# Wider start-up streams, x's splits ahead of the weights' and an earlier bias table in a two-layer decoder step

## The chip, the cores and the metric

The kernel runs on one core of a Trainium2 chip. The metric is the device time of one execution in microseconds (us), the median of several runs; it is compared with the median of the kernel before. All shares and moments below are of one profiled execution and count from its first instruction.

## What is computed

The reference is one inference step of a decoder trunk of two layers on 256 prompt tokens and 8 sample tokens (264 columns in all), model width 1024, in float32. Each layer projects x by one wide matrix, runs three mixers, gates and merges them, and ends with a SwiGLU block:

```python
u = x @ w_in
(q_r, k_r, v_r, g_r, z, xbc, dt_raw, q_c, k_c, v_c, gates) = jnp.split(u, _offsets(IN_SIZES), axis=-1)
# retention on q_r, k_r, v_r; SSD on xbc, dt; sliding-window attention on q_c, k_c, v_c:
bias = rel_bias[_t5_bucket(jnp.maximum(dist, 0))].astype(F32)
logits = jnp.where(mask[None, :, None, None], s + bias, -1e30)
...
mix = (g_a * br_a + g_b * br_b + g_c * br_c) @ w_out
x = _layer_norm(ALPHA * x + mix, ln1_g, ln1_b)
ffn = (jax.nn.silu(x @ w_ffn_gate) * (x @ w_ffn_up)) @ w_ffn_down
x = _layer_norm(ALPHA * x + ffn, ln2_g, ln2_b)
```

The bias of the sliding window is a table over distance, one row of 383 values for each of 8 heads, shared by both layers.

## The kernel before

Everything is held transposed: 128 channels on the partitions, the 264 tokens as columns. To keep float32 accuracy every product is made of three matmuls in a reduced format (`mm3`): a high part times a high part, high times low, low times high. So each weight block and each block of x is first split into a high part, written by ScalarE (`wh`, `xh`), and a remainder, written by VectorE (`wl`, `xl`). A unit of a projection is 128 output channels: 8 blocks of x times 3 matmuls of 264 columns, 24 matmuls, gathered in one PSUM bank.

Weights come by strips of 1 MB (or two halves of 0.5 MB) through SyncE's queue into 4 strip buffers (`strip`); the queue's next strip is issued when a buffer is released by its splits. Small loads, the states and all stores go through GpSimd's queue, in the order of the program.

The start of the program, `load_x`, loads an identity (`cst`), the two halves of the prompt (`xt`) and the sample rows (`xts`). While they travel, TensorE runs 32 matmuls of a constant 128 by 128 tile with itself (`ps_warm`); their result is never read. Then x is transposed block by block (`ps_x`: two transposes of 128 columns and a narrow one for each of 8 blocks; four PSUM banks), and each block is split. The first projections are `w_kv` (2 units) and `w_qc` (4 units), by `halves`: each strip holds four of the eight blocks of x. Behind them come `params` (`ps_par`, `ps_head`), `w_v` (4 units) and `w_qk` (8 units).

`bias_table` is a generator in three pieces: it loads its small inputs; then multiplies the relative bias by a one-hot matrix (`ps_rb`), copies the row to `brow`, makes the sample tokens' bias (`ps_bs`, `bias_s`), stores the row to DRAM (`bias_row`) and spreads it there over 128 rows for each head (`bias`, two transfers of four heads each). `swa`, the window attention, reads `bias` back in a skewed pattern (`bias_t`, two transfers) and adds it to the scores `ps_sc`.

A scheduler that goes by its own timing model sets the order of the instructions on each engine at build time; `high_priority` and `issue_after` in the code are its hints. On the chip each engine then keeps that order. `pump` advances the queue of side work (`bias_table`, `swa` and others) between units.

Of the kernel before, what the change touches and what calls it, by code (L numbers as in the profile page):

```python
# [30 lines left out]
NEG = -1e30  # L31
RSCALE = 128**-0.5

WARM = 32
CONV = 1536

QR, KR, VR, GR, ZZ, XBC, DT, QC, KC, GATE = 0, 512, 1024, 1536, 2048, 3072, 4608, 4624, 5136, 5392
# [69 lines left out]
class Kern:  # L107
# [118 lines left out]
        self.mm(ps, wl, xh, False, last)  # L226

    def xsplit(self, h, l, src):
        self.act(h, src)
        self.sub(l, src, h.bitcast(F32))  # L230

    def gemm(self, w, x, ps, first=True, last=True):

# [6 lines left out]
    def load_x(self):  # L240
        nc, a, cp = self.nc, self.a, self.cp
        keep = _OFF["onehot"][0]
        self.cst = cp.tile([128, keep], F32, name="cst")
        nc.sync.dma_start(self.cst[:, 0:256], a["cst"][:, 0:256])

        self.xb = [self.xp.tile([128, KB, T + 2], F32R, name=f"x{c}") for c in "hl"]
        self.xw = [tuple(t[:, k] for t in self.xb) for k in range(KB)]
        self.x = [(h[:, :T], lo[:, :T]) for h, lo in self.xw]
        xt = [self.T4("xt")[:, :D] for _ in range(2)]
        xs = self.T4("xts")[:NS, :D]  # L250
        nc.sync.dma_start(xt[0], a["x_prompt"][0, 0:128])
        nc.sync.dma_start(xt[1], a["x_prompt"][0, 128:256])
        nc.sync.dma_start(xs, a["x_sample"][:, 0])
        self.neg = cp.tile([128, 128], F32R, name="neg")
        nc.vector.memset(self.neg.bitcast(F32), -1.0 / 128)
        self.par = [None] * DEPTH
        ps = self.pg("ps_warm")
        for _ in range(WARM):
            self.mm(ps[:, :128], self.neg, self.neg)
        bias = self.bias_table()  # L260
        next(bias)
        self.queue.append(bias)
        for k in range(KB):
            ps = self.pm("ps_x")
            for c in range(2):
                self.tr(ps[:, c * 128 : (c + 1) * 128], xt[c][:, k * 128 : (k + 1) * 128])
            self.tr(ps[:, SEQ:T], xs[:, k * 128 : (k + 1) * 128])
            with self.tc.high_priority(400):
                self.xsplit(*self.x[k], ps[:, :T])
        self.pump(1)  # L270
        self.eps = cp.tile([128, 2], F32, name="eps")
        self.alpha = [cp.tile([128, 128], F32R, name=f"al{c}") for c in "hl"]
        h, lo = self.alpha
        self.act(h, self.c("ident"), scale=ALPHA)
        self.stt(lo, self.c("ident"), ALPHA, h.bitcast(F32), ALU.mult, ALU.subtract)
        nc.vector.memset(self.eps[:, 0:1], EPS)
        nc.vector.memset(self.eps[:, 1:2], 4.0 * EPS)
# [37 lines left out]
    def bias_table(self):  # L315

        nc, a = self.nc, self.a
        keep = _OFF["onehot"][0]
        cs0 = self.T2("cs0")[:, : _CST.shape[1] - keep]
        self.ld(cs0, a["cst"][:, keep:])  # L320
        oh, sel = cs0[:32, 0:129], cs0[:8, 129:257]
        rb = self.S([32, 8], "rb")
        self.ld(rb, a["rel_bias"])
        row = self.T2("brow")[:8, :385]
        nc.gpsimd.memset(row[:, :383], NEG)
        self.ld(row[:, 383:385], a["sinks"].rearrange("l h -> h l"))
        yield
        ps = self.pm("ps_rb")
        self.mm(ps[:8, :129], rb, oh)
        nc.vector.tensor_copy(out=row[:, 127:256], in_=ps[:8, :129])  # L330

        self.bias_s = self.cp.tile([128, 131], F32, name="bias_s")
        ps = self.pm("ps_bs")
        self.mm(ps[:, :129], sel, row[:, 127:256])
        self.mm(ps[:, 129:131], sel, row[:, 383:385])
        self.act(self.bias_s, ps[:, :131])

        once = self.dp.tile([8, 383], F32, name="bias_row")
        self.ld(once, row[:, :383])
        self.bias = self.dp.tile([8, 128, 383], F32, name="bias")  # L340
        for h in range(0, 8, 4):
            self.ld(self.bias[h : h + 4], once[h : h + 4].unsqueeze(1).to_broadcast([4, 128, 383]))
        yield


# [210 lines left out]
    def mixers(self, l):  # L556
# [10 lines left out]
        def halves(c0, n, name, pieces, shape):  # L567

            pss = [self.pg("ps_u") for _ in range(n)]
            for i in range(2):  # L570
                raw = self.strip([(0, 128, self.win(l, c0, n * 128)[:, 4 * i : 4 * i + 4])], (4, n * 128), name)
                for u in range(0, n, 2):
                    ws = self.wsplits([pieces(raw, u + v) for v in range(2)], shape)
                    if n == 2:

                        for k in range(4):
                            for v in range(2):
                                x = self.x[4 * i + k]
                                self.mm3(pss[v][:, :T], *(w[:, k] for w in ws[v]), *x, i + k == 0, i == 1 and k == 3)
                        continue  # L580
                    for v in range(2):
                        self.gemm(ws[v], self.x[4 * i : 4 * i + 4], pss[u + v][:, :T], i == 0, i == 1)
# [520 lines left out]
    def swa(self, l):  # L1103
# [28 lines left out]
        for half in range(2):  # L1132
            lgs.append(self.T8("lg")[:, :1536])
            bias = self.T4("bias_t")[:, :1024].rearrange("p (h j) -> p h j", h=4)
            o = self.bias.offset + half * 4 * 128 * 383 + 127
            self.ld(bias, bass.AP(tensor=self.bias.tensor, offset=o, ap=[[382, 128], [128 * 383, 4], [1, 256]]))
            biases.append(bias)
        for t in range(4):

# [538 lines left out]
```

## Time and profile before

| | us |
|---|---|
| median of 3 runs | 1091.47 (1088.8 to 1091.77) |
| the profiled execution | 1088.66 |
| its span, first to last instruction | 1086.9 |
| TensorE busy | 1068.3 (98%) |
| VectorE busy | 840.1 (77%) |
| ScalarE busy | 662.4 (61%) |
| GpSimd busy | 163.4 (15%) |
| TensorE's granted clock, mean share of full speed | 0.997 |

A matmul's busy time includes the way through the array and overlaps the next one's, so the distance between two starts, not the duration, tells the pace. A time in brackets behind a row is the idle time of the engine before it, with what ended it.

### The profile page before, as it was taken

To read this page: it belongs to the slowest core of one execution; us is meant where nothing else is said; L and a number is where in the kernel's file an instruction comes from. 1 tells how busy PE (TensorE), PEld (TensorE's weight loads), DVE (VectorE), ACT (ScalarE), POOL (GpSimd) and SP (SyncE) were. 2 spreads that over 40 slices of the span, in tenths; PEclk is the share of its full clock that TensorE was granted. 3 is DMA by queue.
4 is the path that set the end of the run, shared out by engine and by line. 5 is a ranking of instruction groups with operands and counts; after the bars stand their busy time and mean duration, and the time that the engine had idled before them with its cause. 6 is when DMAs were issued, how large, how long until landed. Compare 5 with 4: busy or idle time off the path is not lost.

```text
span 1086.9 us, 22192 instructions
## 1 busy us (share of the span) xinstructions
PE 1068.3 (98%) x8619; PEld 1029.9 (95%) x8619; DVE 840.1 (77%) x1904; ACT 662.4 (61%) x1332; POOL 163.4 (15%) x248
## 2 busy tenths in 40 slices
PE   9999999999999999999999999999999999999998
PEld 7988998999999999999999899889999999999996
DVE  3588885898868997777599888478886899877654
ACT  3476556667646776665467855366675558666452
POOL 3300012522001011221020001153100000222300
PEclk9999999999999999999999999999999999999999
DMA  9854555994455678899675344669855546989951
GB/s 313 258 175 153 158 145 180 246 273 164 155 194 156 219 247 287 290 312 317 198 254 171 127 156 128 194 160 301 247 183 174 176 149 207 291 286 298 324 183 41
DMA packets 176826, 230.74 MB, mean 212 GB/s; under 512 B 8040, under 2 KB 151984, under 8 KB 176544
## 3 DMA queue, kind: packets, MB, share of 16 engines
q1 hardware_dynamic: 156384, 166.95, 47.6%
q0 software_dynamic: 20272, 62.34, 19.6%
q8 instruction: 68, 1.11, 0.4%
q14 instruction: 38, 0.31, 0.1%
q10 hardware_dynamic: 64, 0.03, 0.0%
HBM read 213.52 MB, written 19.61 MB: 214 GB/s over the span
## 4 chain that ended last, share of the span: by engine, by line
PE 61%; issue 26%; DMA 6%; DVE 3%; POOL 2%; ACT 1%; POOLq 0%; DVEq 0%; ACTq 0%
PE ps_gate L125 12%; PE ps_fg L125 10%; PE ps_fu L125 10%; PE ps_br L125 7%; PE ps_fd L125 6%; PE ps_z L125 5%; PE ps_o L125 4%; PE ps_u L125 4%; DMA bias<-bias_row 2%; DMA rs<-in_state_ret_dram 1%; PE ps_y L125 1%; DVE wl L146 1%; DMA vb<-scr_v 1%; PE ps_var L125 1%; DMA out_dram<-sn 1%
## 5 line engine op out<-in xcount | busy, mean ns | idle before, releaser
L125 PE MATMUL ps_u<-xh,wh 128*128 128x264 f32 x608 | 176.1, 291 | 3.1 <-ACT wh L141 1.8
L125 PE MATMUL ps_u<-xl,wh 128*128 128x264 f32 x608 | 176.4, 290 | 0.0
L125 PE MATMUL ps_u<-xh,wl 128*128 128x264 f32 x608 | 175.6, 291 | 0.1
L125 PEld LDWEIGHTS ps_u<-xh,wh 128*128 128x128 f32 x608 | 116.1, 192 | 6.5 <-ACT wh L141 2.3
L125 PEld LDWEIGHTS ps_u<-xh,wl 128*128 128x128 f32 x608 | 116.5, 192 | 2.1 <-issue 1.7
L125 PEld LDWEIGHTS ps_u<-xl,wh 128*128 128x128 f32 x608 | 116.3, 191 | 1.1 <-issue 0.5
L125 PE MATMUL ps_gate<-xh,wh 128*128 128x264 f32 x384 | 110.1, 290 | 2.2 <-ACT th L141 2.2
L125 PE MATMUL ps_gate<-xl,wh 128*128 128x264 f32 x384 | 109.4, 288 | 0.0
L125 PE MATMUL ps_gate<-xh,wl 128*128 128x264 f32 x384 | 108.9, 288 | 0.0
L125 PE MATMUL ps_fd<-fh,wl 128*128 128x264 f32 x352 | 100.4, 285 | 0.0
L125 PE MATMUL ps_fd<-fh,wh 128*128 128x264 f32 x352 | 100.3, 285 | 0.0
L125 PE MATMUL ps_fd<-fl,wh 128*128 128x264 f32 x352 | 100.0, 284 | 0.0
L125 PE MATMUL ps_fg<-xl,wh 128*128 128x264 f32 x288 | 82.5, 286 | 1.0 <-DVE xl L158 1.0
L169 POOL DMA_DIRECT2D s<-in_state_ssm_dram x32 | 28.8, 900 | 362.4 <-ACT sn L141 229.1
L141 ACT ACTIVATE wh<-w_gate 128x1024 fp32r<-128x1024 f32 x48 | 50.6, 1057 | 53.5 <-PE ps_br L125 19.8
L146 DVE TENSOR_TENSOR wl<-w_fd,wh 128x1024 fp32r<-128x1024 f32 (+1 forms) x48 | 54.2, 1136 | 36.6 <-ACT wh L141 36.5
L125 PE MATMUL ps_fu<-xh,wh 128*128 128x264 f32 x288 | 82.4, 286 | 0.0
L125 PE MATMUL ps_fg<-xh,wh 128*128 128x264 f32 x288 | 82.0, 285 | 0.3 <-DVE v L158 0.3
L125 PE MATMUL ps_fu<-xl,wh 128*128 128x264 f32 x288 | 82.1, 285 | 0.0
L125 PE MATMUL ps_fu<-xh,wl 128*128 128x264 f32 x288 | 81.8, 284 | 0.0
L125 PE MATMUL ps_fg<-xh,wl 128*128 128x264 f32 x288 | 81.7, 284 | 0.0
L141 ACT ACTIVATE wh<-w_fd 128x1024 fp32r<-128x1024 f32 (+1 forms) x48 | 47.1, 986 | 54.8 <-PE ps_fd L125 46.2
(458 smaller groups left out, 3416.0 us busy)
## 6 DMA issues: line engine op xcount, KB each, us to landing
w_gate<-in_w_in_dram SPq DMA_DIRECT2D x24, 1024.0 KB, 5.4
w_fg<-in_w_ffn_gate_dram SPq DMA_DIRECT2D x22, 1024.0 KB, 5.2
w_fu<-in_w_ffn_up_dram SPq DMA_DIRECT2D x22, 1024.0 KB, 6.3
s<-in_state_ssm_dram POOLq DMA_DIRECT2D x32, 512.0 KB, 7.0
w_fd<-in_w_ffn_down_dram SPq DMA_DIRECT2D x16, 1024.0 KB, 8.9
out_dram<-sn POOLq DMA_DIRECT2D x24, 512.0 KB, 7.7
w_qk<-in_w_in_dram SPq DMA_DIRECT2D x8, 1024.0 KB, 9.4
w_xs<-in_w_in_dram SPq DMA_DIRECT2D x8, 1024.0 KB, 5.0
```

The source lines that it names most:

```text
L125: return self.nc.tensor.matmul(out, lhsT, rhs, start=start, stop=stop).ins
L141: i = self.nc.scalar.activation(out=out, in_=in_, func=func, scale=scale, **kw)
L146: return self.nc.vector.tensor_tensor(out=out, in0=a, in1=b, op=op).ins
L169: return self.nc.gpsimd.dma_start(out, in_).ins
```

## The change

Four edits stand together.

- The 32 matmuls of 128 columns become 16 of 512 columns: the moving operand is the same tile four times, by a broadcast access.
- `xsplit` returns its two instructions; those of block 1 of x are kept as `self.after`, and the first split of `halves` is made to stand behind them in the order.
- The generator's second piece is pumped ahead of the last block's transposes, not after all of them, and a third piece is cut off: what makes `bias_s` now comes behind the stores to DRAM.
- `bias` becomes two DRAM tiles of four heads each, so that a load of `bias_t` depends on one of the two stores.

```diff
-WARM = 32
+WARM = 16
...
     def xsplit(self, h, l, src):
-        self.act(h, src)
-        self.sub(l, src, h.bitcast(F32))
+        return self.act(h, src), self.tt(l, src, h.bitcast(F32), ALU.subtract)
...
         for _ in range(WARM):
-            self.mm(ps[:, :128], self.neg, self.neg)
+            self.mm(ps.rearrange("p (a b) -> p a b", a=4), self.neg, self.neg.unsqueeze(1).to_broadcast([128, 4, 128]))
...
         for k in range(KB):
+            if k == KB - 1:
+                self.pump(1)
...
-                self.xsplit(*self.x[k], ps[:, :T])
-        self.pump(1)
+                i = self.xsplit(*self.x[k], ps[:, :T])
+            if k == 1:
+                first = i
+        self.after = first
...
-        self.bias = self.dp.tile([8, 128, 383], F32, name="bias")
-        for h in range(0, 8, 4):
-            self.ld(self.bias[h : h + 4], once[h : h + 4].unsqueeze(1).to_broadcast([4, 128, 383]))
+        self.bias = [self.dp.tile([4, 128, 383], F32, name=f"bias{h}") for h in range(2)]
+        for h in range(2):
+            self.ld(self.bias[h], once[4 * h : 4 * h + 4].unsqueeze(1).to_broadcast([4, 128, 383]))
+        yield
...
-                    ws = self.wsplits([pieces(raw, u + v) for v in range(2)], shape)
+                    with ExitStack() as es:
+                        for j in self.after:
+                            es.enter_context(self.tc.issue_after(j))
+                        ws = self.wsplits([pieces(raw, u + v) for v in range(2)], shape)
+                    self.after = ()
```

The lines on `once` and `bias` now stand ahead of those that make `bias_s`, with the new `yield` between.

TensorE at the start of the program, before (`ps_warm` the constant streams, `ps_x` the transposes of x, `ps_u` the first projections):

```order
L125 MATMUL ps_warm<-neg 128x128 x32
L129 MATMUL ps_x<-cst,xt 128x128 x7
L129 MATMUL ps_x<-cst,xts 128x8 x3
L129 MATMUL ps_x<-cst,xt 128x128
L129 MATMUL ps_x<-cst,xts 128x8
L125 MATMUL ps_u<-xh,wh 128x264 x2
L129 MATMUL ps_x<-cst,xt 128x128 x2
L129 MATMUL ps_x<-cst,xts 128x8
L125 MATMUL ps_u<-xl,wh 128x264
```

The same place now:

```order
L125 MATMUL ps_warm<-neg 128x512 x16
L129 MATMUL ps_x<-cst,xt 128x128 x8
L129 MATMUL ps_x<-cst,xts 128x8 x4
L129 MATMUL ps_x<-cst,xt 128x128 x2
L129 MATMUL ps_x<-cst,xts 128x8
...
L125 MATMUL ps_u<-xh,wh 128x264
L125 MATMUL ps_u<-xl,wh 128x264
L125 MATMUL ps_rb<-cs_111,rb 8x129
```

Seven blocks of x are transposed ahead of the first projection, where four were; the bias row's matmul `ps_rb` is third behind them, where 21 matmuls of `ps_u` stood ahead of it.

ScalarE at the same place, before (`wh` and `xh` are high parts):

```order
L141 ACTIVATE alh<-cst 128x128
L141 ACTIVATE wh<-w_kv 128x512 x4
L141 ACTIVATE xh<-ps_x 128x264 x4
L141 ACTIVATE wh<-w_qc 128x512 x2
L141 ACTIVATE xh<-ps_x 128x264 x4
```

and now:

```order
L141 ACTIVATE alh<-cst 128x128
L141 ACTIVATE xh<-ps_x 128x264 x4
L141 ACTIVATE wh<-w_kv 128x512 x2
L141 ACTIVATE xh<-ps_x 128x264
L141 ACTIVATE wh<-w_kv 128x512 x2
L141 ACTIVATE xh<-ps_x 128x264 x2
L141 ACTIVATE wh<-w_qc 128x512 x4
L141 ACTIVATE xh<-ps_x 128x264
```

The first four blocks of x moved ahead of all weights; VectorE's remainders follow the same order.

GpSimd's queue behind the first loads, before (`bias_t` is the read of the table; `ctok` and `kvs` are the new cache rows on their way out):

```order
L169 DMA bias_row<-brow 8x383
L169 DMA bias<-bias_row 512x1x383 x2
L169 DMA bias_t<-bias 128x4x256 x2
L169 DMA kcache<-in_cache_swa_k_dram 128x8x128
```

and now:

```order
L169 DMA bias_row<-brow 8x383
L169 DMA bias_165<-bias_row 512x1x383
L169 DMA bias_166<-bias_row 512x1x383
L165 DMA out_dram<-ctok 128x128 x2
L165 DMA out_dram<-kvs 8x128 x2
L169 DMA bias_t<-bias_165 128x4x256
L169 DMA bias_t<-bias_166 128x4x256
L169 DMA kcache<-in_cache_swa_k_dram 128x8x128
```

Four stores moved ahead of the reads of the table. SyncE's queue has the same transfers in the same order.

## Rows read from the trace of the kernel before

**Rows 1.** The page, part 1: busy us (share of the span) xinstructions.

```profile
PE 1068.3 (98%) x8619; PEld 1029.9 (95%) x8619; DVE 840.1 (77%) x1904; ACT 662.4 (61%) x1332; POOL 163.4 (15%) x248
```

**Rows 2.** Chain that ended last, by time: start, us, what.

```profile
399.73 2.93 PE ps_fu L125 x24
```

**Rows 3.** Timeline of TensorE, start of the program: start, us, engine, line, operation.

```profile
1.06 7.09 PE L125 MATMUL ps_warm<-neg 128*128 128x128 f32 x32 [1.06 <-DVE neg L255]
7.94 1.72 PE L129 MATMUL ps_x<-cst,xt 128*128 128x128 f32 x7
...
11.95 0.81 PE L125 MATMUL ps_u<-xh,wh 128*128 128x264 f32 x2 [1.27 <-ACT xh L141]
...
24.89 0.42 PE L125 MATMUL ps_u<-xh,wh 128*128 128x264 f32 x1
25.11 0.42 PE L125 MATMUL ps_u<-xl,wh 128*128 128x264 f32 x1
...
25.52 0.29 PE L125 MATMUL ps_u<-xh,wh 128*128 128x264 f32 x1
...
39.14 0.25 PE L129 MATMUL ps_par<-cst,par_rows 100*128 100x100 f32 x1
```

**Rows 4.** Windows: engines' busy us (xinstructions), granted clock, DMA share, GB/s.

```profile
20.00:22.00 2.00, 2.00 (x9) 1.34 (x9) 0.71 (x2) 0.00 (x1) 0.00 (x0) 1.00 1.10 350
687.60:691.00 3.40, 1.33 (x23) 0.93 (x27) 0.81 (x1) 1.44 (x2) 0.87 (x1) 1.00 0.67 200
691.00:694.40 3.40, 3.40 (x28) 3.02 (x25) 0.43 (x1) 0.28 (x1) 0.91 (x2) 0.51 1.12 344
76.70:80.10 3.40, 2.52 (x22) 2.27 (x21) 2.28 (x6) 3.36 (x11) 0.00 (x0) 1.00 0.00 0
```

**Rows 5.** One window, of `ps_u`'s instructions alone (no POOL column).

```profile
11.95:25.50 13.55, 10.54 (x39) 9.00 (x40) 0.00 (x0) 0.00 (x0) 1.00 1.04 331
```

**Rows 6.** Timeline of TensorE, layer 2, as a wait ends at 691 us.

```profile
692.14 0.42 PE L125 MATMUL ps_br<-chl,wl 128*128 128x264 f32 x1
692.36 0.64 PE L125 MATMUL ps_br<-chl,wh 128*128 128x264 f32 x2
```

**Rows 7.** Timeline of TensorE, transposes of the attention weights (`ps_pT`).

```profile
77.03 1.48 PE L129 MATMUL ps_pT<-cst,lg 128*128 128x128 f32 x12
```

**Rows 8.** Timeline of ScalarE, splits at the start.

```profile
9.05 1.15 ACT L141 ACTIVATE wh<-w_kv 128x512 fp32r<-128x512 f32 x2 [5.78 <-DMA w_kv<-in_w_in_dram]
...
11.53 1.22 ACT L141 ACTIVATE xh<-ps_x 128x264 fp32r<-128x264 f32 x4
...
33.32 1.06 ACT L141 ACTIVATE wh<-w_v 128x1024 fp32r<-128x1024 f32 x1 [1.79 <-PE ps_u L125]
```

**Rows 9.** Timeline of VectorE, remainders at the start.

```profile
9.71 2.71 DVE L146 TENSOR_TENSOR wl<-w_kv,wh 128x512 fp32r<-128x512 f32 x4 [6.12 <-ACT wh L141]
12.34 1.45 DVE L146 TENSOR_TENSOR xl<-ps_x,xh 128x264 fp32r<-128x264 f32 x4
```

**Rows 10.** Timeline of GpSimd: issues of the bias table's transfers.

```profile
22.17 0.51 POOL L169 DMA_DIRECT2D bias_row<-brow  x1 [9.54 <-DVE brow L330]
27.53 2.24 POOL L169 DMA_DIRECT2D bias<-bias_row  x2 [4.85 <-DMA bias_row<-brow]
42.65 0.81 POOL L169 DMA_DIRECT2D bias_t<-bias  x1 [12.87 <-issue]
```

**Rows 11.** DMA issues, 0 to 75 us: count, KB each, median us to landing.

```profile
w_v<-in_w_in_dram SPq DMA_DIRECT2D x2, 1024.0 KB, 14.6
bias<-bias_row POOLq DMA_DIRECT2D x2, 766.0 KB, 15.2
xt<-in_x_prompt_dram SPq DMA_DIRECT2D x2, 512.0 KB, 5.5
bias_t<-bias POOLq DMA_DIRECT2D x2, 512.0 KB, 6.3
```

**Rows 12.** DMA by queue, 33 to 44 us: packets, MB, share of 16 engines.

```profile
q1 hardware_dynamic: 1545, 1.56, 51.6%
```

More of the change, by code (lines that the diff above doesn't have):

```diff
@@ L330, in bias_table @@
         nc.vector.tensor_copy(out=row[:, 127:256], in_=ps[:8, :129])
+        once = self.dp.tile([8, 383], F32, name="bias_row")
+        self.ld(once, row[:, :383])
+        self.bias = [self.dp.tile([4, 128, 383], F32, name=f"bias{h}") for h in range(2)]
+        for h in range(2):
+            self.ld(self.bias[h], once[4 * h : 4 * h + 4].unsqueeze(1).to_broadcast([4, 128, 383]))
+        yield
         self.bias_s = self.cp.tile([128, 131], F32, name="bias_s")
@@ L336, in bias_table @@
         self.act(self.bias_s, ps[:, :131])
-        once = self.dp.tile([8, 383], F32, name="bias_row")
-        self.ld(once, row[:, :383])
-        self.bias = self.dp.tile([8, 128, 383], F32, name="bias")
-        for h in range(0, 8, 4):
-            self.ld(self.bias[h : h + 4], once[h : h + 4].unsqueeze(1).to_broadcast([4, 128, 383]))
         yield
@@ L1134, in swa @@
             bias = self.T4("bias_t")[:, :1024].rearrange("p (h j) -> p h j", h=4)
-            o = self.bias.offset + half * 4 * 128 * 383 + 127
-            self.ld(bias, bass.AP(tensor=self.bias.tensor, offset=o, ap=[[382, 128], [128 * 383, 4], [1, 256]]))
+            b = self.bias[half]
+            self.ld(bias, bass.AP(tensor=b.tensor, offset=b.offset + 127, ap=[[382, 128], [128 * 383, 4], [1, 256]]))
             biases.append(bias)
```

## The prediction

> **What bounds the kernel now.** I read the page first: TensorE is busy for 1068.3 of 1086.9 us [rows 1], so a change pays where it shortens TensorE's own row of work or one of its waits. Then the timeline of TensorE from the start of the program, for the distance between starts. In the middle of the program 24 matmuls of 264 columns take 2.93 us, 0.122 us each [rows 2]. In the first 25 us the same matmul starts every 0.22 us, and only at 25.5 us does its duration drop from 0.42 to 0.29 us [rows 3]. The same 0.22 us stands in layer 2 at 692 us [rows 6], in a stretch whose granted clock is given as 0.51 [rows 4]: that is the 1.2 GHz level, and 0.122 us belongs to the 2.4 GHz level. (The clock column reads 1.00 at the start too [rows 4, 5]; the spacing contradicts it, and I go by the spacing.) So all of the start, up to 25.5 us, runs at the low level, the 32 constant streams and the first projections alike. From 11.95 to 25.5 us TensorE gets through 39 matmuls of `ps_u` [rows 5] that would cost 39 × 0.122 = 4.8 us at the high level.
>
> What the engine did before the clock rose: 7.1 us of streams of 128 columns did not raise it; transposes mixed with `ps_u` did not; `ps_u` back to back did, up to 25.5 us. Before 691 us TensorE was busy for only 1.33 of 3.4 us [rows 4], and then it fell.
>
> The last views were ScalarE's and VectorE's timelines, for the splits that the first `ps_u` waits for [rows 8, 9], and the transfers behind them [rows 10 to 12].
>
> **The streams.** 32 streams of 128 columns take 7.09 us, 0.22 us each [rows 3]. A stream of 512 columns at the low level is an estimate from the 264-column spacing: 512 / 264 × 0.22 = 0.43 us, so 16 of them take 6.8 us: from 1.06 to 7.9 us, as now, or less if the clock rises among them. Nothing is lost there. The second half of x, 5.5 us after its issue [rows 11], arrives at about 7.2 us in any case. What changes is that the engine streams columns without pause, as the `ps_u` did that raised the clock. I expect it to rise before 7.9 us.
>
> **The start of the projections.** Now the first `ps_u` starts at 11.95 us, after 1.27 us of waiting for an `xh` [rows 3]; that `xh` stood behind four `wh` of `w_kv`, which ran from 9.05 us, when the weights had landed [rows 8]. After the change: 12 transposes from 7.2 to 7.9 us on, 1.48 us at the high level by the 12 transposes of `ps_pT` [rows 7], 2.7 us at the low one (seven take 1.72 us [rows 3]); then four `xh`, 1.22 us [rows 8], of which the first starts once its own block is transposed; then one `wh` of 0.62 us. That is 8.4 + 1.2 + 0.6 = 10.2 us at best, 10.9 us at worst; I take 10.5 us. The transposes of blocks 4 to 6, now ahead of `ps_u`, wait for PSUM banks that `xl` releases (four take 1.45 us [rows 9]) and end in the same time, so they hide behind the splits.
>
> **From there to the end of `w_qc`.** In both orders exactly 144 matmuls of `ps_u` (48 of `w_kv`, 96 of `w_qc`) stand ahead of `ps_par`, which now starts at 39.14 us [rows 3]. At the high level they take 144 × 0.122 = 17.6 us. Add 0.3 us for `ps_rb`, 0.35 us for the last block's transposes, 0.7 us of waiting for the first `wl` (0.69 us of VectorE, four in 2.71 us [rows 9]) and 0.3 us for later splits: 10.5 + 17.6 + 1.65 = 29.75 us, or **9.4 us earlier**. `ps_bs` moves behind `ps_par` and takes back 0.3 us. The splits keep up: per half strip of `w_qc` ScalarE needs 4 × 0.53 us and VectorE 4 × 0.6 us, against 48 × 0.122 = 5.9 us of matmuls.
>
> **What is late next: `w_v`.** Both strips of `w_v` are there at 27 us (the second is issued at 12.4 us and takes 14.6 us [rows 11]), while its first split runs at 33.32 us, held by TensorE and not by the transfer [rows 8]. After the change that split is wanted at 28 to 29 us. And here the other edit meets it. The bias table's stores, issued at 27.53 us and 15.2 us in flight [rows 10, 11], move up with `ps_rb` to about 18 us, on top of the strips. While they run, SyncE's queue moves 1.56 MB in 11 us [rows 12], 0.14 MB/us, where everything together moves 350 GB/s without them [rows 4]. With 2.8 MB still to come for `w_v` at 19 us (8 us to 27 us at 0.35), the first strip would land between 24 us (no hindrance) and 31 us (0.14 throughout): a wait of 0 to 2 us. I take 1.0 us. It cannot be below nothing.
>
> **The table's own path.** The reads `bias_t` now stand behind four stores of `ctok` and `kvs` on GpSimd. These wait for the first values of `w_v`, so the reads go out at about 38 us instead of 42.65 and land 6.3 us later [rows 10, 11], at 44 to 46 us. The third pair of score matmuls `ps_sc` needs the banks that the first pair's addition frees, and stands 74 matmuls of `ps_u` behind: at about 47 us. The margin is 0 to 3 us; I take a wait of 0.5 us.
>
> **The rest.** Behind about 175 us the two orders agree but for neighbours that changed places; between 45 and 175 us the scheduler wrote the side work in a different order. The same work, the same lengths: 0, with ±1.5 us, the size of the waits of that stretch.
>
> **The sum**: −9.4 + 0.3 + 1.0 + 0.5 = −7.6 us. Against the profiled execution, 1088.66 us, that is 1081.1 us; the median, 1091.47 us, lies 2.8 us above that execution, so I put the median after at 1083.9 us.
>
> **Rivals.** *The clock falls again in the transposes.* Between the streams and the first `ps_u` lie some 3 us in which TensorE only transposes. For it: nothing but transposes would hold the clock there. Against it: from 76.7 to 80.1 us TensorE did 22 matmuls of which 12 are transposes in one row, was busy for 2.52 of 3.40 us, and the granted clock stayed at 1.00 [rows 4, 7]. If it falls, a low stretch follows as at 691 us, 3.4 us [rows 4], or twice that, and gives away half of it: 1.7 to 3.4 us, for 1086 to 1087 us. This is what the Trainium skill says in "TensorE: Matmul & The Clock Gate", Part 4: transposes do not count as busy for the clock. By that rule the sum would be −5 us instead of −7.6; the window at 76.7 us speaks against it, though not purely, since ordinary matmuls lie in it too.
>
> *The streams do not raise the clock*, so the change does not do what it says. Then the transposes take 2.7 us, ScalarE starts `wh` later than now, the first `ps_u` runs at about 12 us at the low level, and the clock rises only behind a dense stretch of `ps_u`, as it did before; with the transposes out of the way I put that at about 17 us instead of 25.5 us: 23 matmuls at 0.22 us, 121 at 0.122 us, 1.5 us of the small things. `ps_par` comes at 33.3 us, 5.8 us earlier; less 1.8 us as above, 1087.5 us.
>
> *The strips are the bound.* If the table's stores hold the queue down for 15 us and `w_v` and `w_qk` all come late, each of the two can cost 2 to 3 us: −9.4 + 0.3 + 5 + 0.5 = −3.6, 1088 us.
>
> *Slower: the table comes late.* If the two stores, fighting with 3.8 MB of strips, take 30 us instead of 15.2, `bias_t` lands near 60 us. VectorE stands at the addition with the `wl` of `w_qk` queued behind it, and TensorE at `ps_sc`. The wait starts to count when the read lands after 47 us and eats the whole gain after 54 us; at 60 us it would be 13 us, less 9 us of gain, 1095 us.
>
> **How the numbers follow.** A measurement of this kernel tells about 0.3%, 3.3 us, from no change: faster means under 1088.2 us. Forecast 0.57 (1083.9, its ends 1080 and 1087); clock falls 0.20 (1086.5); streams idle 0.07 (1087.5); strips bound 0.10 (1088); late table 0.06 (1095). The first four lie mostly under 1088.2: 0.56 + 0.17 + 0.04 + 0.05 = 0.82 faster; the rest of them, 0.12, within; 0.06 slower. The range 1080 to 1088.5 leaves out the late table, a part of the strips, and what is better than the lower ends of the costs.
>
> **What would show it.** The spacing of the `ps_warm` streams falling from 0.43 to 0.22 us among them; `ps_u` starting at 10.5 us with starts 0.122 us apart; `ps_par` near 30 us; no wait of the first `ps_u` of `w_v` over 2 us. Wrong would be a first `ps_u` spacing of 0.22 us (the clock), a wait on `w_v`'s strip (the stores), or a `ps_par` near 30 us with an unchanged span (the gain given back later).

## The result, and the profile after

The median after the change is 1085.88 us (1082.21 to 1092.02) beside 1093.17 us (1088.8 to 1099.89) for the kernel before in the same runs: a ratio of 0.9943, with an interval of 0.9924 to 0.9963. The ratio is taken over all runs of both kernels and not from the two medians, whose quotient is 0.9933. The medians lie 7.3 us apart; the forecast was 1083.9 us in a range of 1080 to 1088.5. The profiled execution took 1083.71 us (span 1081.9 us), 5.0 us less than that of before.

The page, part 1, against [rows 1]: TensorE is busy for 5.3 us less, with the 16 streams fewer, and still for 98% of the span.

```profile
PE 1063.0 (98%) x8603; PEld 1023.0 (95%) x8603; DVE 838.8 (78%) x1904; ACT 661.4 (61%) x1332; POOL 163.8 (15%) x248
```

TensorE's timeline of the kernel after, the same places as [rows 3] (start, us, engine, line, operation, and in brackets the wait ahead of it):

```profile
1.06 6.24 PE L125 MATMUL ps_warm<-neg 128*128 128x512 f32 x16 [1.06 <-DVE neg L254]
7.13 1.03 PE L129 MATMUL ps_x<-cst,xt 128*128 128x128 f32 x8
...
9.27 0.44 PE L129 MATMUL ps_x<-cst,xt 128*128 128x128 f32 x2 [0.76 <-DVE xl L146]
...
10.84 0.39 PE L125 MATMUL ps_u<-xh,wh 128*128 128x264 f32 x1
...
11.82 0.28 PE L125 MATMUL ps_u<-xl,wh 128*128 128x264 f32 x1
11.94 0.28 PE L125 MATMUL ps_u<-xh,wl 128*128 128x264 f32 x1
...
30.29 0.25 PE L129 MATMUL ps_par<-cst,par_rows 100*128 100x100 f32 x1
```

Two `ps_u` behind each other start 0.12 us apart from 11.82 us on (11.82 and 11.94), where before they stood 0.22 us apart up to 25.5 us. The trace's own record of the granted clock rises at 6.0 us, among the streams; in before it rises at 25.47 us. `ps_par`, behind the same 144 `ps_u`, comes at 30.29 instead of 39.14 us: 8.85 us earlier.

ScalarE and GpSimd of the kernel after, against [rows 8] and [rows 10]:

```profile
8.36 1.24 ACT L141 ACTIVATE xh<-ps_x 128x264 fp32r<-128x264 f32 x4 [5.05 <-PE ps_x L129]
...
27.06 1.06 ACT L141 ACTIVATE wh<-w_v 128x1024 fp32r<-128x1024 f32 x1 [3.27 <-PE ps_u L125]
...
13.03 0.51 POOL L169 DMA_DIRECT2D bias_row<-brow  x1
21.28 2.25 POOL L169 DMA_DIRECT2D bias<-bias_row  x2 [7.75 <-DMA bias_row<-brow]
...
39.85 1.56 POOL L169 DMA_DIRECT2D bias_t<-bias  x2
```

The four `xh` now run at 8.36 us, ahead of every `wh`. The first split of `w_v` waits for TensorE's `ps_u`, not for a transfer. The table's stores go out at 21.28 instead of 27.53 us, its reads at 39.85 us.

The 8.85 us do not all last. I took the start of TensorE's n-th matmul behind the streams in each trace (both have 8587 of them) and subtracted: at the 1350th (171.56 us after, 180.17 us before) the kernel after is 8.62 us ahead, at the 1400th (182.58 and 187.94 us) only 5.36 us, at the 4000th 5.24, at the 8500th 4.53 us. So 3.3 us are lost between 171 and 183 us. There TensorE's timeline of the kernel after reads:

```profile
171.56 1.09 PE L129 MATMUL ps_rt<-cst,on 128*128 128x128 f32 x4
173.16 1.48 PE L129 MATMUL ps_rt<-cst,on 128*128 128x128 f32 x4 [0.52 <-DVE gg L146]
174.47 0.27 PE L129 MATMUL ps_craw<-cst,craw 128*36 128x128 f32 x1
...
176.01 0.39 PE L125 MATMUL ps_gate<-xh,wh 128*128 128x264 f32 x1 [1.15 <-ACT th L141]
...
177.00 0.42 PE L125 MATMUL ps_gate<-xh,wh 128*128 128x264 f32 x1
```

And its windows (busy us of each engine, then granted clock, DMA share, GB/s):

```profile
173.20:176.70 3.50, 2.18 (x11) 1.35 (x12) 2.60 (x5) 3.47 (x8) 0.00 (x0) 1.00 0.18 54
176.70:180.10 3.40, 3.40 (x18) 3.32 (x17) 2.54 (x3) 2.04 (x5) 1.93 (x4) 0.50 0.69 262
```

The same place in before:

```profile
180.15 0.27 PE L129 MATMUL ps_rt<-cst,on 128*128 128x128 f32 x1
...
180.38 0.93 PE L129 MATMUL ps_rt<-cst,on 128*128 128x128 f32 x7
...
182.91 0.39 PE L125 MATMUL ps_gate<-xh,wh 128*128 128x264 f32 x1 [1.12 <-ACT th L141]
```

From the first of retention's eight transposes `ps_rt` to the `ps_craw` behind them 2.9 us pass after the change (171.56 to 174.47 us) and 1.2 us before (180.15 to 181.39 us, with one `ps_gate` among them). The `ps_gate` behind them waits for ScalarE's `th` in both kernels, 1.15 and 1.12 us, so this wait is no part of the loss. Then, after the change alone, 3.4 us run at the low level: a `ps_gate` takes 0.42 us again, as `ps_u` did at the start of before.

The order of TensorE's row says why the transposes wait: between the last `ps_qkv` of the retention's norm and the first `ps_rt` stand 19 `ps_gate` after the change and 38 before. ScalarE writes the eight inputs `on` of the transposes, with a split of `w_gate` between the fifth and the sixth (kernel after):

```profile
170.40 1.86 ACT L141 ACTIVATE on<-ps_ro,nb,rrr 128x128 f32<-128x128 f32 x5 [0.77 <-DVE nb L158]
172.13 1.07 ACT L141 ACTIVATE wh<-w_gate 128x1024 fp32r<-128x1024 f32 x1
173.08 1.18 ACT L141 ACTIVATE on<-ps_ro,nb,rrr 128x128 f32<-128x128 f32 x3
```

The last `on` ends at 174.26 us, 5 us behind that `ps_qkv` (169.03 us), and 19 `ps_gate` of 0.12 us cover 2.3 us of them. Of the 3.3 us, 1.7 us are this waiting inside the row of `ps_rt` (2.9 less 1.2 us), and 1.6 us are the clock. The kernel with the streams alone, below, has the same waits without a fall there, and loses 1.7 us between the same two columns.

### The profile page after: what moved, and what is told of

The parts are those of the page before. It is cut to its first block, busy times and chain, and to the rows that moved or that the text cites. A ratio compares the mean times of both kernels' runs of the same rounds, so it can differ in the third digit from the quotient of the medians.

```text
span 1081.9 us, 22158 instructions
## 1 busy us (share of the span) xinstructions
PE 1063.0 (98%) x8603; PEld 1023.0 (95%) x8603; DVE 838.8 (78%) x1904; ACT 661.4 (61%) x1332; POOL 163.8 (15%) x248
## 4 chain that ended last, share of the span: by engine, by line
PE 79%; issue 12%; DVE 4%; ACT 2%; DMA 2%; POOL 1%; ACTq 0%; POOLq 0%
PE ps_u L125 12%; PE ps_gate L125 12%; PE ps_fd L125 12%; PE ps_fu L125 10%; PE ps_fg L125 10%; PE ps_br L125 6%; PE ps_z L125 5%; PE ps_o L125 5%; DVE wl L146 1%; PE ps_y L125 1%; ACT wh L141 1%; DMA rs<-in_state_ret_dram 1%; PE ps_var L125 1%; PE ps_st L125 1%; PE ps_warm L125 1%
## 5 line engine op out<-in xcount | busy, mean ns | idle before, releaser
L125 PE MATMUL ps_u<-xl,wh 128*128 128x264 f32 x608 | 173.4, 287 | 0.0
L125 PE MATMUL ps_u<-xh,wl 128*128 128x264 f32 x608 | 173.0, 288 | 0.0
## 6 DMA issues: line engine op xcount, KB each, us to landing
w_fd<-in_w_ffn_down_dram SPq DMA_DIRECT2D x16, 1024.0 KB, 11.5
```

The lines of the kernel that those rows point to most:

```text
L125: return self.nc.tensor.matmul(out, lhsT, rhs, start=start, stop=stop).ins
```

## The experiments

Theory A: the gain is the clock, which unbroken streams raise ahead of x; x's splits first add about 1 us, the bias part nothing; what is lost later is lost through the order of the side work. The rivals are named in each expectation. One table for all: how far ahead of before (us) each kernel is, at TensorE's n-th matmul behind its streams (behind its added transposes too), with the ratio to before and its interval.

```
n =                    100    350   1350   1400   4000   8000   ratio [interval]
before at, us        30.05  59.95 180.17 187.94 511.48 1008.90
after                 8.43   8.12   8.62   5.36   5.24   4.52   0.9943 [0.9924, 0.9963]
e1_streams_alone      7.50   6.10   5.80   4.09   3.79   3.20   0.9995 [0.9969, 1.0021]
e2_old_streams        3.60   2.75   2.22   2.22   1.90   1.25   0.9982 [0.9958, 1.0007]
e3_old_bias           8.40   6.99   6.84   7.21   7.23   7.89   0.9927 [0.9904, 0.9951]
e4_no_x_first         7.25   5.95   6.43   2.02   1.75   1.10   0.9980 [0.9956, 1.0004]
e6_eight              6.15   6.02   4.08   4.23   0.28  -0.53   1.0012 [0.9990, 1.0034]
e7_later_rt           7.10   6.79   7.27   8.97   3.33   3.82   0.9967 [0.9938, 0.9996]
e9_eighteen           8.36   6.77   6.47   6.47   6.55   4.14   0.9959 [0.9934, 0.9983]
e10_after_again       6.44   6.14   6.68   3.44   2.63   1.02   0.9944 [0.9922, 0.9965]
e11_twelve            7.41   6.63   5.17   5.16   5.20   3.53   0.9946 [0.9918, 0.9974]
e12_pump_earlier      8.48   7.19   7.06   7.41   7.27   6.72   0.9930 [0.9903, 0.9957]
```

The columns come from one profile each, the ratio from several runs; where the two differ, the low stretches of the clock fell elsewhere in the profiled run than in the others. An estimate takes these stretches out: each run's time multiplied by its mean granted clock, since a stretch at half the clock gives away about half of its length (1.6 of 3.4 us above; the start, ahead of the first rise on record, counts as 1.00 in that mean). By it the mean of a kernel lies under that of before, in the same set of runs, by 3.5 us for e1, 2.1 for e2, 6.4 for e3, 3.1 for e4, 5.6 for e10 (the kernel after) and 7.3 for e12, each to within 0.8 to 1.6 us. So the streams alone and the order alone are each worth something, and together about what the whole change is worth (3.5 and 2.1 beside 5.6 us).

### The streams alone

```
-WARM = 32
+WARM = 16
-            self.mm(ps[:, :128], self.neg, self.neg)
+            self.mm(ps.rearrange("p (a b) -> p a b", a=4), self.neg, self.neg.unsqueeze(1).to_broadcast([128, 4, 128]))
```

> The kernel before with only the sixteen streams of 512 columns in place of its 32 of 128; its order of splits and of the bias part is as before. Theory A (the gain is the clock, which the unbroken long streams raise among themselves): the spacing of the streams falls from about 0.43 to 0.22 us, the transposes and ps_u behind them stand at the high level, the first ps_u still comes at 11.5 to 12 us because xh still stands behind wh of w_kv, and ps_par stands at about 31 us (39.14 before, 30.29 after): 8 of the 8.85 us, ratio about 0.994. Rival B (the gain is the order, x's splits ahead of the weights'): ps_par at 36 us or later, ratio 0.998 to 1.000. Rival C (the clock rises in the streams but falls again where TensorE stands idle between the first ps_u, since it waits longer for splits here than after): ps_u spacing of 0.22 us returns, ps_par at 33 to 36 us.

The clock rises at 6.58 us and stays up to 1075 us. The first `ps_u` starts at 9.73 us, earlier than A's 11.5 to 12. `ps_par` stands at 31.62 us, 7.5 us earlier than before: of the gain at the start, nearly all belongs to the streams. TensorE's timeline shows what is still missing against after, a first `ps_u` that waits for its `xh`, and then one `ps_u` at a time between transposes:

```profile
9.73 0.39 PE L125 MATMUL ps_u<-xh,wh 128*128 128x264 f32 x1 [0.97 <-ACT xh L141]
```

B and C fall for the start. But the ratio is 0.9995, which is B's, and here A was wrong: 7.5 us at 30 us are 3.8 us at 511 us, and no more than about 2 us in the median, which is not clear of no change. The larger losses are at places that the change does not touch: 1 us at 50 us (below) and 1.7 us at `ps_rt`, where 19 `ps_gate` stand as in after. What the median lacks of the profile's 3.2 us is the clock of the other runs: the mean granted clock of its twelve runs is 0.9938, that of before's runs beside them 0.9955. Why it falls more often here is not shown.

### The order alone

```
-WARM = 16
+WARM = 32
-            self.mm(ps.rearrange("p (a b) -> p a b", a=4), self.neg, self.neg.unsqueeze(1).to_broadcast([128, 4, 128]))
+            self.mm(ps[:, :128], self.neg, self.neg)
```

> The kernel after with the 32 streams of 128 columns as before; the order of splits and the bias part as after. Theory A: the streams run at 0.22 us each and do not raise the clock, the transposes take about twice as long as after (2.7 instead of 1.5 us), the first ps_u comes at about 12 us with 0.22 us spacing, the clock rises behind a dense row of ps_u at about 17 us, ps_par at about 33 us; ratio against before 0.995 to 0.998. Rival B (order alone): ps_par at 30 to 31 us, like the kernel after, ratio 0.994.

The clock rises at 19.69 us (A had about 17) instead of 25.47, behind a row of `ps_u` that starts at 11.63 us, and the kernel is 3.6 us ahead at the 100th matmul (only 72 `ps_u` stand ahead of `ps_par` in this order, so its moment does not compare). The order alone gives under half of the start, by letting the same clock rise sooner. B falls.

### Without the bias part

```
-            if k == KB - 1:
-                self.pump(1)
 ...
+        self.pump(1)
```

with the table again one tile and its stores behind `ps_bs`, as in before.

> The kernel after with its bias part put back: the row's matmul behind all transposes, ps_bs ahead of the stores, one table. Theory A: this part is worth nothing at the start; ps_par at 30.3 us within 0.5, the clock as after, ratio as that of after within what can be told (0.3 per cent). Rival D (the earlier stores of the table matter): a wait at the score matmuls or at the strip of w_v that after does not have, 1 to 3 us, or, the other way, w_v's strips land earlier than 28.6 us. Theory A also says that the 3.3 us which after gives back between 171 and 180 us come from how the scheduler ordered the side work there: if this kernel's order there is another, that loss may move or be gone, with the start unchanged.

`ps_par` at 30.73 us, 8.40 us ahead at the 100th matmul: the bias part gives nothing at the start, and there is no wait ahead of attention's matmuls. The second strip of `w_v` lands at 27.42 us for 28.61 in after, the other way that D names, but the splits of `w_v` wait for `ps_u` and not for it. D falls. What the kernel has is another order: 37 `ps_gate` ahead of `ps_rt`, no loss at 171 to 190 us, and 7.2 us still there at 511 us. (Its profile loses 5.8 us behind the table's last column, to a wait of 2.76 us and 6.8 us of low clock at 1034 us.)

### Without the splits of x first

```
-        self.after = first
```

> The kernel after without the rule that the first splits of the weights wait in order for the split of x's block 1. Theory A: the first ps_u about 1 us later than after (11.5 to 12 us instead of 10.84), ps_par at 31 to 31.5 us, ratio 0.994 to 0.996. Rival B (the order is the gain): ps_par at 35 us or later, ratio 0.998 or above. If the clock needs TensorE busy without long pauses after the streams, the longer wait for xh here lets it fall: a spacing of 0.22 us among the first ps_u shows that.

The first `ps_u` starts at 9.97 us, earlier than after and than A's 11.5 to 12, but behind it they again stand one by one between transposes; `ps_par` comes at 31.38 us, in A's range, 7.25 us ahead at the 100th matmul. So the rule is worth 1.2 us at the start. No low stretch follows there. The ratio, 0.998, is outside A's range and at the edge of B's, for two reasons that the trace shows. The first is attention's `ps_sc` at 50 us, in this kernel:

```profile
50.53 0.92 PE L125 MATMUL ps_sc<-kv,qc 64*128 64x128 f32 x4
...
51.69 0.92 PE L125 MATMUL ps_sc<-kv,qc 64*128 64x128 f32 x4
```

and in the kernel after:

```profile
49.64 0.93 PE L125 MATMUL ps_sc<-kv,qc 64*128 64x128 f32 x8
```

They work on 64 partitions, one half of the heads on the lower, the other on the upper 64. Eight in a row take as long as four alone: side by side the two halves run at once, with a `ps_u` between them one after the other. That is the 1.1 us by which this kernel, e1, e3, e9 and e12 fall behind between the 300th and the 350th matmul, and after does not. (The Trainium skill, "TensorE: Matmul & The Clock Gate", Part 3, says that matmuls on separate row groups run concurrently; these rows agree.) The second is the clock: 6.8 us at the low level from 177.33 us, behind the same waits at `ps_rt` as in after. (Another 3.4 us at 689 us before has as well, at 691 us.)

### The transposes of retention later

```
+        if l == 0:
+            yield
         pr, pr3 = self.gg, gg3
```

> The kernel after with one more step of the side work ahead of retention's transposes ps_rt in layer 1 alone, so that 51 matmuls of 264 columns stand between the last ps_qkv and the first ps_rt, where after has 19 and before 38. Theory A (of what after gains at the start, 3.3 us are given back between 171 and 180 us, because the transposes stand too early in TensorE's row: 1.6 us of waits, and 1.7 us of the low clock that follows them): the waits of ps_rt and of the ps_gate behind it go, the granted clock shows no fall there in the profile, the offset against before stays at about -8.5 us up to 570 us, and the median comes 1.5 to 3.3 us under that of after, ratio 0.991 to 0.993. Rival E (the place does not matter, the same time is lost at the next side work or at the branch that uses the result): offset at 200 us -5 to -6 us as in after, ratio 0.994.

With 51 matmuls ahead of `ps_rt` the loss is gone: 7.27 us ahead at the 1350th matmul, 8.97 at the 1400th, and 9.3 at 252 us. That much of A holds. But the gain does not last: at 257 us TensorE waits, and VectorE's column (the third) in the windows of that stretch is full.

```profile
256.93 0.72 PE L125 MATMUL ps_br<-rhl,wh 128*128 128x264 f32 x2 [1.94 <-DVE zt L158]
```

```profile
248.00:254.00 6.00, 6.00 (x51) 5.09 (x51) 6.00 (x19) 3.69 (x9) 1.74 (x4) 1.00 0.66 209
254.00:260.00 6.00, 4.06 (x23) 3.87 (x22) 6.00 (x14) 2.66 (x6) 0.00 (x0) 0.75 0.47 154
```

The whole side work stands behind its old place, VectorE is busy without a break from 242 to 260 us, and TensorE loses 1.94 us there, 1.34 and 1.49 us at 284 to 287 us, and a low stretch from 257.0 to 260.4 us: 6 us in all. The ratio, 0.9967, is outside A's range and worse than E's 0.994; E had the place right: the time is lost at the branch that uses the result. Pushing side work back does not cure it.

### What raises and lowers the clock

Four kernels serve this, the first two for their clock alone. First the kernel after with 48 transposes of a constant tile behind the streams:

```
+        for _ in range(48):
+            self.tr(ps[:, :128], self.neg.bitcast(F32))
```

> The kernel after with 48 more transposes of the constant tile behind the sixteen streams; the time of this kernel is read for its clock alone. At the high level 48 take about 6 us (0.128 us each), at the low level twice that. Theory A as the traces so far bear it out (transposes hold the clock): it rises at 6 to 7 us, the 48 end at about 13.5 us, all of them and the 24 of x behind them start 0.13 us apart or less, ps_u 0.12 us apart. Rival F (transposes do not count as work for the clock, which is what the Trainium skill says in TensorE: Matmul & The Clock Gate, Part 4): the clock record shows 0.5 within the transposes or right behind them, their spacing goes to about 0.22 us, and the first ps_u stand 0.22 us apart.

```profile
7.12 5.40 PE L129 MATMUL ps_warm<-cst,neg 128*128 128x128 f32 x48
...
14.92 0.39 PE L125 MATMUL ps_u<-xh,wh 128*128 128x264 f32 x1
```

```profile
7.10:12.30 5.20, 5.20 (x49) 5.18 (x48) 0.00 (x0) 0.00 (x0) 3.85 (x7) 1.00 1.08 368
12.30:14.90 2.60, 2.60 (x18) 1.67 (x15) 1.37 (x3) 1.84 (x5) 1.16 (x5) 1.00 1.07 387
```

From 7.12 to 14.92 us TensorE did nothing but transposes, 0.11 us each to the last of the 48 (5.24 us to the next row at 12.36 us), and the clock record stays at 1.00 from 5.95 to 53.7 us. Rival F falls: transposes without pauses hold the clock. The Trainium skill, "TensorE: Matmul & The Clock Gate", Part 4, says that transposes do not count as busy for the clock; the measurement decides otherwise for the transposes of this kernel. Whether transposes alone would raise it was not tried.

Then 64 streams of 128 columns:

```
-WARM = 16
+WARM = 64
-            self.mm(ps.rearrange("p (a b) -> p a b", a=4), self.neg, self.neg.unsqueeze(1).to_broadcast([128, 4, 128]))
+            self.mm(ps[:, :128], self.neg, self.neg)
```

> The kernel after with 64 streams of 128 columns, twice the number of the kernel before, which keep TensorE busy for 14 us; read for its clock alone. Theory A (it is the unbroken columns of the long streams that raise the clock; streams of 128 columns, 0.22 us each where their columns alone would fill half of that, do not): no rise in the 14 us, the spacing stays 0.22 us to the last, the clock rises only behind a row of ps_u, at 22 to 27 us. Rival H (the 32 streams of before were only too few, or too late in their row): the spacing falls to about 0.11 us within the 64, between 7 and 15 us.

```profile
1.06 13.91 PE L125 MATMUL ps_warm<-neg 128*128 128x128 f32 x64 [1.06 <-DVE neg L254]
...
23.12 0.28 PE L125 MATMUL ps_u<-xl,wh 128*128 128x264 f32 x1
```

64 in 13.9 us are 0.22 us each to the end: no rise in 14 us in which TensorE is busy throughout. It rises at 23.1 us, 3.5 us after the first `ps_u` at 19.66, where the duration drops to 0.28 us. A holds, H falls. Both kinds of stream load weights once each; by the 264 columns of a `ps_u` in 0.22 us at this level, 128 columns fill 0.11 of a short stream's 0.22 us, and 512 fill a long one's 0.43 us (an estimate). Whether it is the missing columns or the denser weight loads that keep the short streams at the low level, this run does not separate.

Then half of the streams:

```
-WARM = 16
+WARM = 8
```

> The kernel after with 8 streams of 512 columns instead of 16: 3.4 us of them, from 1.06 to 4.5 us, then TensorE stands idle until x's second half is there at about 7 us. Theory A (the row of unbroken columns up to the transposes raises the clock): no rise before the transposes; these run at the low level, and it rises within the first dense ps_u, at 12 to 18 us; ps_par at 32 to 34 us, ratio 0.995 to 0.998. Rival G (3.4 us of streams are enough, the rest of the sixteen does nothing): a rise at 5 to 7 us all the same, ps_par at 30 to 31 us, ratio 0.992 to 0.995.

```profile
7.83 0.66 PE L129 MATMUL ps_x<-cst,xt 128*128 128x128 f32 x4 [2.18 <-DMA xt<-in_x_prompt_dram]
```

```profile
5.50:8.80 3.30, 1.12 (x9) 0.74 (x8) 0.00 (x0) 0.13 (x1) 1.51 (x3) 1.00 0.99 322
8.90:15.60 6.70, 6.01 (x23) 4.29 (x24) 5.11 (x13) 5.29 (x13) 4.51 (x10) 0.50 1.08 388
```

Neither side had it right. The 3.4 us of streams do raise the clock, at 5.46 us (A had said no), but TensorE then waits 2.18 us for x's second half, and from 8.87 to 15.7 us it runs at the low level (G had said no). The streams have to reach up to the data. The ratio is 1.0012, outside both ranges: the 6.15 us that are left at the start are gone by 511 us, through a wait of 1.85 us and low clock at 176 us, and a wait of 2.21 us and low clock at 261 us. The mean granted clock of its runs is 0.9922, that of before's beside them 0.9968.

And twelve:

```
-WARM = 16
+WARM = 12
```

> The kernel after with 12 streams of 512 columns instead of 16: they end at about 6 us, then TensorE waits about 1 us for x's second half. Between the last ps_qkv and the first ps_rt stand 38 matmuls here, as in before. Theory A (the streams must reach up to the transposes, as the 8 streams showed, where the clock rose at 5.46 and fell again at 8.87 us): a rise at 5 to 6 us, and a fall among the transposes in part of the runs; ps_par at 31 to 33 us, ratio 0.993 to 0.996. Rival L (12 are as good as 16): no fall, ps_par at 30 to 30.5 us, and with the better order ratio 0.991 to 0.993.

The rise is at 4.22 us, x's second half is waited for 1.07 us, and the clock falls at 11.04 us for 3.4 us; `ps_par` at 31.30 us, ratio 0.9946. So A expected the fall and the ratio, and had the rise later (5 to 6 us). The next run shows that sixteen streams can end too early as well.

### The kernel after again, and with two streams more

The kernel after without any edit:

> The kernel after once more, for a second profile and for runs beside those of the other kernels. Theory A: the waits at ps_rt and the ps_gate behind it (0.5 and 1.15 us) and the 19 matmuls are there again, since the order is the same; offset at 170 us about -8.5 us. Whether the clock falls at 176 us again is open: theory A' says that the fall follows from those waits and comes in most profiles; rival K says that the moment at which the chip looks decides, and it comes in some only, so that the offset at 200 us is -5.3 with a fall and -7 without. The same holds for the transposes of x at 8 to 11 us.

This profile begins otherwise than the first one of the same kernel:

```profile
1.06 5.57 PE L125 MATMUL ps_warm<-neg 128*128 128x512 f32 x16 [1.06 <-DVE neg L254]
...
8.00 0.66 PE L129 MATMUL ps_x<-cst,xt 128*128 128x128 f32 x4 [0.94 <-DMA xt<-in_x_prompt_dram]
...
9.76 0.44 PE L129 MATMUL ps_x<-cst,xt 128*128 128x128 f32 x2 [0.76 <-DVE xl L146]
...
11.66 0.42 PE L125 MATMUL ps_u<-xl,wh 128*128 128x264 f32 x1
```

```profile
8.00:11.40 3.40, 2.64 (x18) 1.82 (x18) 2.13 (x6) 2.55 (x8) 2.67 (x6) 1.00 1.08 374
11.40:14.80 3.40, 3.40 (x14) 2.74 (x15) 3.01 (x7) 2.30 (x7) 2.34 (x6) 0.50 1.09 392
```

The clock rises at 4.58 us instead of 6.0, and falls at 11.4 us for 3.4 us, after a stretch of transposes with pauses in which TensorE was busy for 2.64 of 3.40 us. That is the prediction's rival of the falling clock, in the very kernel. In the profiles of kernels with 12 or more long streams the rise stands at 4.22, 4.41 and 4.58 us (e11, e7, e10) and a fall follows at 11.0 to 11.4 us; or at 5.66 to 7.25 us (e9, e5, after, e1, e4, e3, e12) and none follows. In those three profiles the streams, at the high level sooner, also end sooner, at 5.5 to 6.6 us instead of 7.3 to 7.9, and TensorE waits 1.07, 0.35 and 0.94 us for x's second half, for which the others do not wait. Whether the early rise or that wait leads to the fall is not separated. The fall costs about 1.5 us here: 6.44 us ahead at the 100th matmul instead of 8.43, of which 0.5 us is the first `ps_u`, at 11.33 instead of 10.84 us.

The waits at `ps_rt` are there again, 0.52 and 1.16 us, and the low stretch behind them too, from 178.66 us: 6.68 us ahead become 3.44. Of the four profiles with 19 `ps_gate` ahead of `ps_rt` three show a fall there (after, e10, e4) and one does not (e1); of the nine with 37 to 51 (before, e2, e3, e5, e7, e8, e9, e11, e12) none does. (e6 is a case by itself: 55 matmuls stand there, and its clock falls at 176 us, ahead of `ps_rt` and behind a `ps_gate` that waits 1.85 us.) So A' holds for the most part, with K's chance in it.

Now two streams more:

```
-WARM = 16
+WARM = 18
```

> The kernel after with 18 streams of 512 columns instead of 16. The start costs at most 0.3 us more (two streams at the high level are 0.44 us, part of it ahead of x's second half). But in the order that the scheduler writes, 38 matmuls of 264 columns stand between the last ps_qkv and retention's first ps_rt of layer 1, as in before, where after has 19. Theory A (what after gives back at 171 to 180 us comes from those 19): no wait of ps_rt, offset against before at 200 us equal to that at 150 us within 0.5 us, about -7 (the score matmuls ps_sc stand apart here as in the kernel without the x-first rule, 1 us), ratio 0.991 to 0.994. Rival J (two streams more are nothing, the loss comes by itself wherever TensorE runs earlier): offset at 200 us -5 us or less, ratio 0.994 to 0.996.

This changes nothing at the start (8.36 us ahead at the 100th matmul), and puts 38 `ps_gate` ahead of `ps_rt`, since the scheduler's tally of TensorE's time is another:

```profile
173.68 0.27 PE L129 MATMUL ps_rt<-cst,on 128*128 128x128 f32 x1
...
173.91 0.93 PE L129 MATMUL ps_rt<-cst,on 128*128 128x128 f32 x7
...
176.43 0.39 PE L125 MATMUL ps_gate<-xh,wh 128*128 128x264 f32 x1 [1.12 <-ACT th L141]
```

`ps_rt` does not wait, the `ps_gate` behind it waits as in before, the clock does not fall, and the kernel is 6.47 us ahead on both sides: A's mechanism is shown in the profile, and J's offset of −5 us or less did not come. The ratio, 0.9959, is all the same not better than after's, and in J's range instead of A's. In the profile 1.1 us went at `ps_sc`; the waits for a `wh` and a `wl` at 75 to 78 us are 0.97 and 1.03 us long, where after has 0.78 and 0.44; and 2.2 us went between 570 and 700 us, where the clock fell for 6.8 us at 684.9 us. The mean granted clock of its runs is 0.9947, that of before's beside them 0.9958.

### The bias row one block earlier

```
-            if k == KB - 1:
+            if k == 6:
                 self.pump(1)
```

> The kernel after with the bias row one block of x earlier (ahead of the transposes of block 6 instead of block 7) and all else as it is. In the order this puts 37 matmuls of 264 columns between the last ps_qkv and the first ps_rt of layer 1, as in the kernel with the old bias part, instead of 19; the score matmuls ps_sc stand apart by one ps_u, as there. Theory A (what separates the kernels now is the order of the side work and where the clock falls, not the bias path): no loss between 171 and 190 us, offset against before at 200 us -6.5 to -7.5 us, ratio 0.991 to 0.994, like the kernel with the old bias part (0.9927). Rival M (the old bias path itself was worth something): ratio 0.994 to 0.996 in spite of the order, or a wait ahead of ps_sc at 48 to 52 us that the kernel with the old bias part does not have.

The order has 37 `ps_gate` ahead of `ps_rt`, all eight of which run in one row at 173.11 us without a wait (the `ps_gate` behind them waits 0.85 us). 7.06 us ahead at the 1350th matmul, 7.41 at the 1400th, 6.72 at the 8000th; median 1082.58 us, ratio 0.9930. It has the new bias path and the ratio of the kernel with the old one, and no wait ahead of `ps_sc`, so nothing speaks for M, though the interval reaches into its range. By their ratios e3 and e12 are the fastest, 0.16 and 0.13% under the kernel after; the intervals overlap, so that this is not more than likely. With the clock taken out e12 is 7.3 us ahead and the kernel after 5.6: the 1.7 us between them are what the waiting inside `ps_rt` costs in the traces, but no more than their errors.

## Why the prediction was right, step by step

**The streams** were right. The clock rises among them in every profile with 12 or more long streams, the engine loses nothing, and their effect on the start stands alone in e1. The reason named, columns without pause, holds against the 64 short streams, whose denser weight loads are not separated from it.

**The start of the projections.** First `ps_u` at 10.84 us for 10.5. The difference is the transposes of blocks 4 to 6: the prediction had them hide behind the splits; they stand ahead of the first `ps_u`, behind a wait of 0.76 us for `xl`, and take from 9.27 to 10.84 us.

**To the end of `w_qc`.** From the first `ps_u` to `ps_par` 19.45 us for a predicted 19.25. With the late start that makes 8.85 us instead of 9.4.

**`w_v`** was costed at 1.0 us and cost nothing: the split at 27.06 us waits for `ps_u`. The step that failed is the moment of the table's stores. From the issue of the small transfer `bias_row` to theirs 8.25 us passed, where before 5.36 did [rows 10], so they went out at 21.28 and not at 18 us. And they hindered the strips less than was reckoned: from 21.28 us to the landing of `w_v`'s second strip at 28.61 us SyncE's queue moved 2.24 MB, 0.31 MB/us, where the prediction took 0.14 [rows 12] as the worst. The two strips took 14.5 us to land in the median, by the DMA issues of 10 to 32 us, where before they took 14.6 [rows 11].

**The table's path** was costed at 0.5 us and cost nothing: the reads go out at 39.85 us for 38, the third pair of `ps_sc` stands at 49.64 us for 47.

**The rest** was put at 0 ± 1.5 us. This term was mis-sized: 3.3 us lost between 171 and 183 us, 1.7 us in the row of `ps_rt` and 1.6 us by the clock. The prediction said that the orders agree behind 175 us but for neighbours, and costed the stretch from 45 to 175 us by its work, not by what stands between a producer and its consumer. The count was there to be read ahead of time: 19 `ps_gate` instead of 38 between `ps_qkv` and `ps_rt`.

**The sum.** In the profile, −7.6 us became −4.5 us at the 8500th matmul: 0.55 us less at the start, 1.5 us of waits that did not come, 3.3 us lost at `ps_rt`, and 0.8 us lost behind that: −7.6 + 0.55 − 1.5 + 3.3 + 0.8 = −4.45. That 0.8 us is the rest of larger moves: 1.6 us go between 510 and 640 us and 0.7 us at 769.9 us, where a `ps_u` waits 0.45 us, and 1.5 us come back at 690 us, because before's clock fell there [rows 4] and after's did not, behind the same waits of `ps_rso` (2.12 and 0.51 us in before, 2.14 and 0.49 in after). That is luck of the two profiles. The two medians lie 7.3 us apart, which is nearer to the forecast than its terms deserve, and that too is luck. They hold what the clock does in all executions: the profiled one of before lies 4.5 us under its median of these runs (1093.17 less 1088.66), that of after 2.2 us. The forecast time itself, 1083.9 us, is 2.0 us under the measured median.

**The rivals.** The falling clock is no separate case but one that comes in part of the executions, at about 1.5 us a time, near the 1.7 us of its lower bound. Transposes without pauses did not bring it (5.95 to 14.92 us in e5); transposes with pauses did, in part of the profiles. The streams that do nothing, the strips as the bound, and the late table did not occur.

## What to carry to other kernels

A dense run of long streams up to the moment at which the first data lands is worth what the first projections lose at the low clock, here 7.5 us at the start; short streams with a weight load each did not raise the clock at all, and streams that end before the data give a part back (8 of them: 6.15 us). But a gain at the start pays only as far as the rest of the program lets it through: after any edit that shifts TensorE's row, count what stands between each chain's producer and its consumer in the new order, because a scheduler that works by its own tally will move side work that the edit never named. Here kernels that were 7.1 to 8.5 us ahead behind the start ended at ratios from 0.9927 to 0.9995. The traces put a part of that on such orders; another part is how often the clock fell in their runs, and why it did so more in some is open.

## What the runs showed that I had not expected

- The moment at which the clock rises differs between executions of the same instructions, from 4.2 to 7.3 us, and with it when the streams end and whether a low stretch follows. (The Trainium skill, "TensorE: Matmul & The Clock Gate", Part 1, says that the chip's watch runs freely and does not begin with the kernel; these rows agree.)
- Pauses of 0.5 to 1.2 us, with TensorE busy for 62 to 78% of 3.4 to 3.5 us, were followed by a fall (8.0 to 11.4 us in e10, 173.2 to 176.7 us in after); before was busy for 74% of 3.4 us at 76.7 us [rows 4] and none followed, and e1, with the same waits at `ps_rt` as after, kept the high level. The busy share alone does not tell.
- The spread of this kernel's times goes with the mean granted clock: the five runs of after at 0.998 lie between 1082.21 and 1083.71 us, the three at 0.992 and 0.993 between 1091.04 and 1092.02 us.
- Two groups of matmuls on 64 partitions each cost 0.93 us side by side and twice 0.92 us apart, so one foreign matmul between them cost 1.1 us.
